# Row tiles and raw weights in buffers of their own, and the second pair's weights split on VectorE

## The chip, the cores and the metric

The kernel runs on one core of a Trainium2 chip. The metric is the device time of one execution in microseconds (us), the median of three runs. The engines are called as in the profile: PE (TensorE matmuls), PEld (TensorE weight loads), DVE (VectorE), ACT (ScalarE), POOL (GpSimd) and SP (SyncE, here only a queue that issues DMAs). "L739" is line 739 of the kernel before; the changed kernel is two or three lines longer from L475 on, so that its L742 is the same line.

## The reference

One layer of a hybrid decoder on 1024 tokens of 1024 channels, all float32. What is computed first matters here:

```python
h = rms_norm(x, pre_mix_norm[l])
proj = h @ w_in[l]
z, xbc, dt_raw, sb_qkv, nsa_q, nsa_kv, nsa_gate, merge_gate = jnp.split(proj, split_points(), axis=-1)
```

with

```python
y = xf * lax.rsqrt(jnp.mean(xf * xf, axis=-1, keepdims=True) + NORM_EPS)
```

Behind it come three token mixers (a state space scan, a stick-breaking attention and a sparse attention), a gated sum, an output projection, a second RMS norm and a gated feed-forward network (FFN) with a short causal convolution:

```python
x = x + rms_norm(mixed @ w_out[l], post_mix_norm[l])
h = rms_norm(x, pre_ffn_norm[l])
u = causal_dwconv(h @ ffn_w_up[l], ffn_conv_w[l], ffn_conv_b[l])
f = (jax.nn.gelu(gate, approximate=True) * val) @ ffn_w_down[l]
```

## The kernel before, in words

**Products in two parts.** Every float32 operand of a large product is split into a rounded high part (`ACT Copy` into a float32r tile, names ending in `hi`) and a low rest (a `subtract` on DVE or POOL, names ending in `lo`). A product is three matmuls: high by high, high by low, low by high.

**The start.** The tokens are worked in two halves h = 0, 1 of 512. SP loads the columns of x (`x<-in_xT`, channels on partitions, eight tiles of a half), the first two chunks of token-major weights (`traw<-in_wtm`, four parts each) and the eight row tiles of x (`row_load`, `uhi<-in_xr` and `ulo<-in_xr`, 128 tokens of 1024 channels each), which serve only for the sums of squares: ACT squares a row tile in place with a running sum (`square`, L483). Four row tiles make the factor 1/rms of one half (`factor`; `rt` and `rb` on ACT and DVE), which PE transposes into a bank (`factor_rows`, four 128x128 matmuls on `rb`). DVE multiplies the half's columns by it (`norm`, L544), ACT rounds (`high`, L547) and DVE subtracts (`low`, L550). Meanwhile PE makes the token-major products of half 0 from columns that carry only the channel gain (`four_tiles`); `hooks` places the transposes between these matmuls: half 0's at (k, n) = (3, 0) of the second chunk, half 1's at (7, 2). Then come the products of half 1, which need its normed columns. These parts are pinned to the order in which they are written.

**Gate unit and pairs.** Next come one gate unit (`load_w`, 128 output channels, L301 to L308) and 24 units of the state space mixer in twelve pairs (`ssm_units`). A pair is done with seven products instead of eight (a Strassen scheme): `weights7` loads two raw weight tiles of 128x1024 (`wraw`, rows a11|a12 and a21|a22), and builds from them the high and low parts of seven combinations: `whi, wlo` (products 1 and 2), `ahi, alo` (product 4), and the sums `uf`, rounded to `uhi, ulo` (products 3 and 6, 5 and 7). `eng` says which engine does the eight adds and subtracts: the gate unit and the first pair use DVE, all other pairs POOL. On the other operand, `combos` makes four sums of the normed columns for each k (DVE, L695 to L698), and 16 splits round them (ACT, L738) and subtract (DVE, L739): products 6, 7, 5 and 4 in this order. The banks are named `dense` (two), `ps_s` (two), `ps_t` (two), `ps_o` and `ps_b`. A pair's results are combined on DVE (L769 to L780), run through a four-tap convolution (ACT L341, DVE L345 and L347), a SiLU (ACT L760), and stored (`s_d<-o`).

**Buffers.** The raw weight tile is taken in turn from two buffers of the pool `w` and one of a pool that the caller gives (`turn`, L655 to L659): two of three come from `w`, the third from `wx`. Load_w uses the two of `w` as well. The same counter runs on in the FFN, where the units from 5 on are pairs again and then the down projection uses `weights7`. A DMA into a buffer waits until its last reader is through; SP issues in order, so a DMA that waits holds all behind it.

**What sets the order.** Apart from the pinned start, a scheduler with a timing model places the instructions on each engine when the kernel is built; `issue_after` (through `behind`) keeps an instruction behind a given other.

## Time and profile before

| what | value |
| --- | --- |
| median of 3 runs | 2199.31 us (2198.98 to 2203.28) |
| profiled execution, its own time | 2196.05 us |
| span of the profiled execution | 2194.3 us |
| PE busy | 2142.0 us, 98% of the span |
| DVE, ACT, POOL busy | 1349.8, 1207.4, 1212.0 us |
| granted TensorE clock | 0.996 of full speed on average |
| PE busy from 0 to 50 us, 50 to 100, 100 to 150 | 43.64, 47.45, 47.92 us |
| the same from 150 to 200 us, 200 to 250, 250 to 300 | 50.00, 49.63, 49.78 us |

The span is what the profiler sees from the first instruction to the last; the execution's own time holds 1.75 us more (2196.05 less 2194.3). A row of a timeline gives the start, the duration, the engine and line, the operation with `out<-in`, and, in brackets, the idle time of the engine ahead of it and what ended it. A list of waits gives us in total, times, and the longest.

### The profile page before, as it was taken

How to read it: one execution, taken by the hardware profiler on the slowest of the kernel's cores; microseconds unless marked ns; L12 is line 12 of the kernel's file. 1: busy time of each engine (PE TensorE's matmuls, PEld its weight loads, DVE VectorE, ACT ScalarE, POOL GpSimd, SP SyncE). 2: the span in 40 equal slices, each digit the busy share in tenths (PEclk: the TensorE clock that was granted, in tenths of full speed). 3: DMA queues.
4: the chain of work that ended last, by engine and by line, in shares of the span. 5: the costliest groups of instructions: out<-in, count | busy, mean ns of one | idle time of the engine just before them, and what ended most of it. 6: DMA issues, size and time to landing. Idle time of an engine off the chain costs nothing.

```text
span 2194.3 us, 30439 instructions
## 1 busy us (share of the span) xinstructions
PE 2142.0 (98%) x10701; PEld 1714.8 (78%) x10701; DVE 1349.8 (62%) x2492; ACT 1207.4 (55%) x2286; POOL 1212.0 (55%) x1075
## 2 busy tenths in 40 slices
PE   8999999999999999999999999999999999999997
PEld 8777879866676678888877777887788888878886
DVE  7855554256656515566547877328776767676776
ACT  6544443457857745676775554236555544475634
POOL 0566642146746743443335686648777777766733
PEclk9999999999999999999999999999999999999999
DMA  7233342321121011212336432335322323255432
GB/s 262 79 114 110 113 130 66 101 77 39 53 78 39 18 57 39 77 54 95 126 116 218 155 104 78 118 113 193 110 82 77 111 96 120 97 194 175 149 116 106
DMA packets 127562, 233.55 MB, mean 106 GB/s; under 512 B 29840, under 2 KB 43952, under 8 KB 127408
## 3 DMA queue, kind: packets, MB, share of 16 engines
q1 hardware_dynamic: 124720, 229.02, 31.6%
q10 hardware_dynamic: 2688, 2.59, 0.3%
q8 instruction: 84, 1.38, 0.3%
q14 instruction: 70, 0.57, 0.1%
HBM read 170.11 MB, written 61.44 MB: 106 GB/s over the span
## 4 chain that ended last, share of the span: by engine, by line
PE 79%; DVE 7%; ACT 5%; issue 4%; DMA 3%; POOL 2%; SPq 0%; DVEq 0%; ACTq 0%; POOLq 0%
PE dense L235 51%; PE ps_s L235 10%; PE ps_t L235 6%; PE ps_o L235 6%; PE ps_b L235 4%; PE psn L235 3%; DMA ulo<-in_xr 1%; ACT wT L1145 1%; DVE u L345 0%; DVE mx L1117 0%; POOL wlo L308 0%; DVE o L345 0%; DVE o L347 0%; DVE x L1826 0%; DMA lo<-m_d 0%
## 5 line engine op out<-in xcount | busy, mean ns | idle before, releaser
L308 POOL TENSOR_TENSOR wlo<-wraw,whi 128x256 fp32r<-128x256 f32 x300 | 238.1, 825 | 212.5 <-ACT whi L303 202.4
L235 PE MATMUL dense<-h_hi,whi 128*128 128x512 f32 x656 | 264.0, 402 | 2.1 <-DVE kk L912 2.1
L235 PE MATMUL dense<-h_hi,wlo 128*128 128x512 f32 x656 | 257.3, 392 | 0.0
L235 PE MATMUL dense<-h_lo,whi 128*128 128x512 f32 x656 | 257.2, 392 | 0.0
L1156 POOL TENSOR_TENSOR wT_lo<-wT,wT_hi 128x512 fp32r<-128x512 f32 x132 | 168.2, 1288 | 70.9 <-ACT wT_hi L1155 56.7
L235 PE MATMUL dense<-x,uhi 128*128 128x512 f32 x600 | 191.7, 391 | 1.9 <-ACT x L748 1.9
L235 PE MATMUL dense<-hi,wlo 128*128 128x512 f32 x448 | 176.4, 395 | 0.1
L235 PE MATMUL dense<-lo,whi 128*128 128x512 f32 x448 | 174.9, 391 | 1.1 <-POOL lo L1845 1.1
L235 PE MATMUL dense<-hi,whi 128*128 128x512 f32 x448 | 174.7, 390 | 0.4 <-ACT whi L303 0.4
L675 POOL TENSOR_TENSOR ulo<-uf,uhi 128x1024 fp32r<-128x1024 f32 x36 | 87.1, 2420 | 116.5 <-ACT uhi L674 116.5
L235 PEld LDWEIGHTS dense<-h_hi,wlo 128*128 128x128 f32 x656 | 123.5, 188 | 27.2 <-POOL wlo L666 0.2
L235 PEld LDWEIGHTS dense<-h_hi,whi 128*128 128x128 f32 x656 | 124.0, 189 | 25.4 <-issue 2.5
L235 PEld LDWEIGHTS dense<-h_lo,whi 128*128 128x128 f32 x656 | 123.9, 189 | 22.9
L303 ACT ACTIVATE whi<-wraw 128x1024 fp32r<-128x1024 f32 x76 | 80.4, 1058 | 111.1 <-PE dense L235 87.4
L235 PEld LDWEIGHTS dense<-x,uhi 128*128 128x128 f32 x600 | 112.4, 188 | 27.3 <-ACT x L748 3.2
L1379 POOL TENSOR_TENSOR s_lo<-sa,s_hi 128x512 fp32r<-128x512 f32 (+2 forms) x48 | 53.9, 1124 | 132.6 <-ACT s_hi L1378 132.6
L345 DVE SCALAR_TENSOR_TENSOR u<-dense,pv,u 128x510 f32<-128x510 f32 (+1 forms) x140 | 103.5, 742 | 32.3 <-ACT u L341 32.1
L1117 DVE TENSOR_REDUCE mx<-ps_t 128x1 f32<-128x384 f32 (+3 forms) x192 | 97.9, 519 | 35.2 <-PE ps_t L235 33.5
L1145 ACT ACTIVATE wT<-ps_s 128x512 f32<-128x512 f32 x132 | 78.3, 596 | 53.0 <-PE ps_s L235 48.6
L678 POOL TENSOR_TENSOR ulo<-uf,uhi 128x1024 fp32r<-128x1024 f32 x36 | 86.6, 2404 | 31.4 <-ACT uhi L677 29.9
L235 PE MATMUL dense<-x,ulo 128*128 128x512 f32 x264 | 103.2, 391 | 0.0
L666 POOL TENSOR_TENSOR wlo<-wraw,whi 128x1024 fp32r<-128x1024 f32 x36 | 88.3, 2455 | 24.3 <-ACT whi L665 24.2
(584 smaller groups left out, 6172.1 us busy)
## 6 DMA issues: line engine op xcount, KB each, us to landing
wraw<-in_wfm SPq DMA_DIRECT2D x62, 512.0 KB, 3.8
wraw<-in_wup SPq DMA_DIRECT2D x48, 512.0 KB, 3.7
lo<-m_d SPq DMA_DIRECT2D x58, 256.0 KB, 3.3
g_d<-gate_e SPq DMA_DIRECT2D x48, 256.0 KB, 2.0
s_d<-o SPq DMA_DIRECT2D x48, 256.0 KB, 2.1
m_d<-u SPq DMA_DIRECT2D x44, 256.0 KB, 2.0
row<-g_d SPq DMA_DIRECT2D x36, 256.0 KB, 3.9
row<-s_d SPq DMA_DIRECT2D x32, 256.0 KB, 5.0
```

The source lines that it names most:

```text
L235: return pin(f(*a, **k), in_order)
L303: act(hi, raw, AF.Copy)
L308: eng.tensor_tensor(lo[:, s], raw[:, s], fl(hi[:, s]), op=OP.subtract)
L345: V.scalar_tensor_tensor(o[:, d:], ps[:, :512 - d], taps[d], o[:, d:], op0=OP.mult, op1=OP.add)
L666: eng.tensor_tensor(wlo, raws[0], fl(whi), op=OP.subtract)
L675: eng.tensor_tensor(l24, f24, fl(h24), op=OP.subtract)
L678: eng.tensor_tensor(l31, f31, fl(h31), op=OP.subtract)
L1117: V.tensor_reduce(mx[:, h, a, n:n + 1], pm[:, :w], axis=AX, op=OP.max)
L1145: act(w.rearrange("p h q -> p (h q)"), pz, AF.Exp)
L1156: P.tensor_tensor(lo, wf, fl(hi), op=OP.subtract)
L1379: (P if SB_SLO else V).tensor_tensor(s_lo[:, c0:], a[:, c0:], fl(s_hi[:, c0:]), op=OP.subtract)
```

## The change

Four things are edited, and the scheduler places the rest anew.

1. **Row tiles.** The eight row tiles went to `uhi` and `ulo` in turn (two buffers each), so that rows 4 to 7 waited for the squares of rows 0 to 3. Now rows 0 and 1 go to `uhi`, 2 and 3 to `ulo`, 4 to `uf0`, 5 to `uf1`, 6 to the `wraw` of the pool wx0, and only row 7 takes a used `uhi`.
2. **Raw token-major weights.** `TM_RAW`, the number of their buffers, goes from 3 to 5; the tile `q_out`, which took room in the same pool, is gone, and its two uses take `ulo` and `uhi`. The fourth part of chunk 1 is loaded ahead of row 7 and not behind it. Its split on ACT and DVE stands ahead of the squares of rows 6 and 7, which moved into `first_rows`; the hook of half 1's transposes goes from (7, 2) to (7, 0).
3. **Second pair's weights.** For the second pair (u0 = 4) `weights7` runs on DVE and not on POOL, and behind the last of the 16 splits, whose subtracts are now in `lows`.
4. **Ring.** `turn` is set to 2 behind the first pair, so that the second pair's first raw tile takes the buffer of wx0. The counter is one lower from there on, in the FFN too.

```diff
-TM_RAW = 3
+TM_RAW = 5
...
-        x = wx0.tile([128, DM], F32, name=("uhi", "ulo")[t // 2 % 2])
+        name = ("uhi", "uhi", "ulo", "ulo", "uf0", "uf1", "wraw", "uhi")[t]
+        x = wx0.tile([128, DM], F32, name=name, bufs=2 if name in ("uhi", "ulo") else 1)
...
-        if t in (3, 7):
+        if t in (3, 6):
             with tc.issue_after(loads[-1].ins):
-                raw1.append(tm_raw(1, 2 + t // 4, tmw))
+                raw1.append(tm_raw(1, t // 3 + 1, tmw))
...
-    def q_tile(name=None):
-        if name:
-            return wx0.tile([128, DM], F32, name=name).rearrange("p (t c) -> p t c", t=4)
-        return tmw.tile([128, 4, 256], F32, name="q_out", bufs=1)
+    def q_tile(name):
+        return wx0.tile([128, DM], F32, name=name).rearrange("p (t c) -> p t c", t=4)
...
     def first_rows():
         rows.append(factor_rows(rb, ps_s))
-        for k in range(4):
+        for k in range(3):
             norm(0, k)
         chunk_weights(1, 3)
+        norm(0, 3)
+        for t in (6, 7):
+            square(t)
         late.append(factor(1)[1])
         norm(0, 4)
...
-    qs = [q_tile()]
+    qs = [q_tile("ulo")]
...
-    for t in range(4, 8):
+    for t in (4, 5):
         square(t)
-    pss = four_tiles(1, tm1, 0, (ps_o, ps_d, ps_d, ps_b), {(3, 0): first_rows, (7, 2): second_rows})
+    pss = four_tiles(1, tm1, 0, (ps_o, ps_d, ps_d, ps_b), {(3, 0): first_rows, (7, 0): second_rows})
...
-    qs.append(q_tile())
+    qs.append(q_tile("uhi"))
...
             first_w = weights7(wx, A["wfm"][U_SSM], A["wfm"][U_SSM + 1], 512, V)
+        turn[0] = 2
...
-                V.tensor_tensor(lo, t, fl(hi), op=OP.subtract)
+                lows.append(V.tensor_tensor(lo, t, fl(hi), op=OP.subtract))
...
-            with behind(columns_in, highs[-1]) if q == 0 else nullcontext():
-                w = weights7(wx, A["wfm"][U_SSM + u0], A["wfm"][U_SSM + u0 + 1], 512) if u0 else first_w
+            with behind(columns_in, highs[-1], lows[-1]) if q == 0 else nullcontext():
+                w = weights7(wx, A["wfm"][U_SSM + u0], A["wfm"][U_SSM + u0 + 1], 512, V if u0 == 4 else P) if u0 else first_w
```

On ACT, in the start, behind the transposed factor `rb` of half 0: before, four squares (`uhi` and `ulo` hold row tiles) and then the split of the last part of chunk 1 (`thi`):

```order
L517 ACTIVATE rb<-rt 128x512
L483 ACTIVATE uhi,stat<-uhi 128x1024 x2
L483 ACTIVATE ulo,stat<-ulo 128x1024 x2
L416 ACTIVATE thi<-traw 128x512
L269 ACTIVATE rt<-stat,eps 128x4
L271 ACTIVATE rt<-rt 128x4
L517 ACTIVATE rb<-rt 128x512
```

and now (`uf_161`, `uf_163` and `wraw` hold the row tiles 4, 5 and 6):

```order
L518 ACTIVATE rb<-rt 128x512
L484 ACTIVATE uf_161,stat<-uf_161 128x1024
L484 ACTIVATE uf_163,stat<-uf_163 128x1024
L416 ACTIVATE thi<-traw 128x512
L484 ACTIVATE wraw,stat<-wraw 128x1024
L484 ACTIVATE uhi,stat<-uhi 128x1024
L269 ACTIVATE rt<-stat,eps 128x4
L271 ACTIVATE rt<-rt 128x4
L518 ACTIVATE rb<-rt 128x512
```

The split moved ahead of the last two squares; nothing else moved on ACT there.

On DVE, behind the 16 splits of the pairs' columns (L739, now L742), before:

```order
L739 TENSOR_TENSOR x<-x 128x512 x16
L744 CAST rtab<-tab 128x256
L769 TENSOR_TENSOR ps_s<-ps_s,x 128x512
L343 COPY halo<-ps_s 128x3
L345 SCALAR_TENSOR_TENSOR o<-ps_s,pv,o 128x511
L345 SCALAR_TENSOR_TENSOR o<-ps_s,pv,o 128x510
L345 SCALAR_TENSOR_TENSOR o<-ps_s,pv,o 128x509
L777 TENSOR_TENSOR x<-ps_t,x 128x512
L778 TENSOR_TENSOR ps_o<-ps_o,x 128x512
```

and now (`wlo`, `uf_1082`, `uf_1083` and `alo` are the second pair's weights):

```order
L742 TENSOR_TENSOR x<-x 128x512 x16
L747 CAST rtab<-tab 128x256
L668 TENSOR_TENSOR wlo<-wraw,whi 128x1024
L673 TENSOR_TENSOR uf_1082<-wraw 128x512
L678 TENSOR_TENSOR uf_1082<-wraw 128x512
L772 TENSOR_TENSOR ps_s<-ps_s,x 128x512
L674 TENSOR_TENSOR uf_1083<-uf_1082,wraw 128x512
L675 TENSOR_TENSOR uf_1083<-uf_1083,wraw 128x512
L343 COPY halo<-ps_s 128x3
L345 SCALAR_TENSOR_TENSOR o<-ps_s,pv,o 128x511
L780 TENSOR_TENSOR x<-ps_t,x 128x512
L682 TENSOR_TENSOR alo<-wraw,ahi 128x512
```

Six of the second pair's eight operations stand between the splits and the first pair's combination and convolution; the other two (`ulo`) follow further down, one behind the convolution of `ps_o` and one ahead of that of `dense`.

On POOL, at the head of its work, before (`uf_1082` and `uf_1083` are the second pair's sums, `uf_1220` the third's):

```order
L671 TENSOR_TENSOR uf_1082<-wraw 128x512
L676 TENSOR_TENSOR uf_1082<-wraw 128x512
L672 TENSOR_TENSOR uf_1083<-uf_1082,wraw 128x512
L666 TENSOR_TENSOR wlo<-wraw,whi 128x1024
L673 TENSOR_TENSOR uf_1083<-uf_1083,wraw 128x512
L666 TENSOR_TENSOR wlo<-wraw,whi 128x1024
L680 TENSOR_TENSOR alo<-wraw,ahi 128x512
```

and now:

```order
L668 TENSOR_TENSOR wlo<-wraw,whi 128x1024 x2
L682 TENSOR_TENSOR alo<-wraw,ahi 128x512
L673 TENSOR_TENSOR uf_1220<-wraw 128x512
L678 TENSOR_TENSOR uf_1220<-wraw 128x512
L674 TENSOR_TENSOR uf_1221<-uf_1220,wraw 128x512
```

The second pair's operations are gone from POOL; it begins with the `wlo` of the third and of the fourth pair. On PE the first pair's product 4 (`ps_o<-x,ahi`, on the last four splits) and its product 6 (`dense<-x,uhi`) now follow product 7 (`ps_t<-x,uhi`) at once; before, most of the second pair's product 1 stood ahead of them, and the second pair's product 2 among them. In the FFN the first pairs' raw tiles also change places: unit 5's second tile now comes from the pool `w` behind the single units' weights, where before it came from `wx`; the four sums of unit 5 on POOL stand behind the last single unit's `wlo`, where the first of them had stood ahead of 24 of these.

## Prediction

> **What bounds the kernel now.** I read the page's busy times first, then the list of PE's waits and the chain of waits over the first 300 us (all edits but the ring lie there), then the timelines of SP, ACT, DVE, POOL and PE. The page:
>
> ```profile
> PE 2142.0 (98%) x10701; PEld 1714.8 (78%) x10701; DVE 1349.8 (62%) x2492; ACT 1207.4 (55%) x2286; POOL 1212.0 (55%) x1075
> ```
>
> PE bounds the whole. The change removes no matmul, so it can win only idle time of PE: 52 us in the span, of which the places it touches hold a few. PE's waits up to 260 us (total, times, longest):
>
> ```profile
> PE dense L235 <- ACT x L748: 2.5, 3, 1.3
> PE ps_s L235 <- ACT rb L517: 1.8, 1, 1.8
> ```
>
> The second lies in the start; of the first, 0.77 lies at the first pairs, beside two waits for DVE that are shown below.
>
> The chain of waits in the start (start, duration, what):
>
> ```profile
> 12.52 8.75 DMA ulo<-in_xr
> ...
> 22.47 5.78 DMA ulo<-in_xr
> ...
> 28.28 1.15 ACT ulo L483 x2
> 29.43 0.53 ACT thi L416
> ...
> 29.98 0.70 DVE tlo L417
> ...
> 31.23 0.71 PE dense L235 x6
> ...
> 33.00 0.45 PE ps_s L235 x4
> ...
> 33.48 2.06 DVE x L544 x3
> ```
>
> So the end of the row stage hangs on row 7 (landed 28.25), its square, then the split of the last weight part (1.2 us on ACT and DVE), which PE needs, and the transposes at 33.00, behind half of k = 7. From there the norm at 33.48 leads to PE's first matmul of half 1:
>
> ```profile
> 34.94 0.39 PE L235 MATMUL ps_t<-thi,h_hi 128*128 128x256 f32 x1 [0.80 <-ACT h_hi L547]
> ```
>
> That is 1.46 us behind the norm's start. I measure the first term there.
>
> **Term 1, row tiles and raw buffers.** SP's row for rows 4 and 5:
>
> ```profile
> 18.48 1.61 SPq L449 DMA_DIRECT2D uhi<-in_xr  x2
> ```
>
> Rows 4 and 5 were held to 18.48 by the squares of rows 0 and 1, and rows 6 and 7 behind them by those of 2 and 3; now they are issued as soon as earlier transfers land. But the transfers are near their limit (last column GB/s):
>
> ```profile
> 8.00:10.00 2.00, 2.00 (x19) 2.00 (x18) 2.00 (x4) 1.64 (x4) 0.00 (x0) 1.00 1.00 368
> 14.00:16.00 2.00, 2.00 (x19) 2.00 (x19) 0.75 (x2) 0.55 (x1) 0.00 (x0) 1.00 1.01 296
> ```
>
> Behind row 3 (landed 21.27) come weight part 3, rows 4 to 6, part 4 and row 7: 2.6 MB, 7.1 us at 368 GB/s, so row 7 lands no earlier than about 27.3 to 28.2 even when dips like the one to 296 are filled. What is won is the order on ACT. `rb` of both halves, and PE's transposes of half 0:
>
> ```profile
> 23.64 0.63 ACT L517 ACTIVATE rb<-rt 128x512 f32<-128x512 f32 x1
> 31.51 0.63 ACT L517 ACTIVATE rb<-rt 128x512 f32<-128x512 f32 x1 [1.13 <-DVE rt L274]
> 25.03 0.63 PE L235 MATMUL ps_s<-ident,rb 128*128 128x128 f32 x4 [1.83 <-ACT rb L517]
> ```
>
> I let rows 0 to 3 come 0.4 us earlier (0 to 0.7, the dip at 14 to 16: 72 of 368 GB/s over 4 us), so ACT is free at 23.9. Squares 4 and 5 (1.15 us each by the row at 28.28, and a tenth between) end near 26.4, part 4 is there at about 26.5, its split and squares 6 and 7 end near 29.5, and `rb` of half 1 follows in 1.9 us (2.7 from 29.43 to 32.14, less 0.8 of the split on ACT and DVE) at 31.4. PE, no longer held by that split, goes from its transposes at 24.6 through 48 matmuls of 0.118 to k = 7 at 30.7 and waits 0.7 us; the transposes end near 31.9 and the norm starts there, against 33.48. Term 1: **1.5 us** won. Bounds: 0.2 when part 4 lands only at 27.7 and both squares queue behind its split; 2.5 when everything lands early and PE waits for nothing. I take the value nearer the upper one because ACT's seven squares and splits, not the transfers, come out last. The hook's move costs nothing unless `rb` is late: then all of k = 7 (12 matmuls, 1.4 us) is behind the wait and not half of it; this is in the 0.2. Both `q_out` uses now hold a buffer of `ulo` and `uhi` until they are stored. The last store (ACT, issued near 58) must land before the first pair's second `uhi`; by the rows it takes 4.0 us, which makes ACT 1 to 2 us late there, most of it hidden by the idle 1.26 us ahead of the gate's sigmoid. Without that cover the splits' high parts come 2 us later, which term 2's bound holds.
>
> ```profile
> q_d<-uhi ACTq DMA_DIRECT2D x1, 512.0 KB, 4.0
> 64.44 0.60 ACT L277 ACTIVATE gate_e<-dense 128x512 f32<-128x512 f32 x1 [1.26 <-PE dense L235]
> ```
>
> **Term 2, the second pair's weights.** On POOL they ran through DVE's 16 splits:
>
> ```profile
> 67.18 5.30 POOL L671 TENSOR_TENSOR uf<-wraw 128x512 f32<-128x512 f32 x1 [66.67 <-DVE ulo L678]
> 80.37 2.83 POOL L666 TENSOR_TENSOR wlo<-wraw,whi 128x1024 fp32r<-128x1024 f32 x1
> 65.87 1.23 DVE L678 TENSOR_TENSOR ulo<-uf,uhi 128x1024 fp32r<-128x1024 f32 x1
> 67.61 3.70 DVE L739 TENSOR_TENSOR x<-x 128x512 fp32r<-128x512 f32 x6
> 71.75 14.42 DVE L739 TENSOR_TENSOR x<-x 128x512 fp32r<-128x512 f32 x10 [0.43 <-ACT x L738]
> 74.22 1.14 ACT L738 ACTIVATE x<-x 128x512 fp32r<-128x512 f32 x2
> 75.26 1.05 ACT L665 ACTIVATE whi<-wraw 128x1024 fp32r<-128x1024 f32 x1
> ```
>
> Alone, six splits take 3.70 us, 0.62 each; with POOL at work, ten take 14.42, 8.2 us too long. POOL's first add took 5.30 us, until DVE had paused at 71.3. From there they take turns, one whole instruction each. The Trainium skill's page "SBUF — State Buffer", section "Who interferes with whom", says that a DVE instruction with two SBUF inputs and a GpSimd one that reads SBUF exclude each other for the whole instruction, whichever issues first; the trace agrees, with splits of 1.4 us on average here.
>
> PE paid for it three times:
>
> ```profile
> 81.88 0.39 PE L235 MATMUL ps_s<-h_lo,whi 128*128 128x512 f32 x1
> 83.81 0.49 PE L235 MATMUL ps_o<-x,ahi 128*128 128x512 f32 x1 [1.54 <-DVE x L739]
> ...
> 96.20 0.39 PE L235 MATMUL dense<-x,ulo 128*128 128x512 f32 x1
> 97.60 0.47 PE L235 MATMUL ps_o<-x,ahi 128*128 128x512 f32 x1 [1.00 <-DVE o L345]
> ...
> 100.21 0.39 PE L235 MATMUL ps_o<-x,alo 128*128 128x512 f32 x1
> 101.37 0.50 PE L235 MATMUL dense<-h_hi,uhi 128*128 128x512 f32 x1 [0.77 <-ACT x L748]
> ```
>
> A matmul here starts 0.23 us behind the one ahead, so these starts are 1.70, 1.17 and 0.93 late: 3.8 us. In the changed order, in times of before (term 1 taken off): ACT's high parts set the pace of the splits up to the 12th, near 75.4. POOL's only operation then is the third pair's `wlo` (2.83 in turns, some 2.4 alone as the `ulo` below), which starts behind `whi` near 76.3 and blocks one split; the 13th ends near 79.4, the 16th near 81.2, against 86.2. Product 4 now stands right behind product 7 and wants the 13th near 78.8 and one more split every 0.7 us: it waits 0.65 us. By the row at 67.18, where POOL waited out six splits, DVE would lose nothing and PE wait 0; at the worst the splits slip by the 2 us above and PE waits 2.6.
>
> Behind the splits DVE has the eight operations: 3 of 1024 columns at 1.23 us and 5 of 512 at 0.62, 6.8 us, of which six stand ahead of the convolutions. Counting on in steps of 0.6 to 0.75, `wlo` ends at 82.7 (PE wants it at 85.2, behind products 4 and 6), the first combination at 84.5, the convolution of `ps_s` at 89.7 and of `ps_o` at 92.0. PE, 12 matmuls or 2.75 us for a product, wants `ps_s` again at 92.4 and `ps_o` at 95.2. So these 6.8 us lie beside PE's work with 2.7 and 3.2 us to spare; without that cover each is a us of PE for a us of DVE. The convolutions read PSUM and do not take turns with POOL: this `ulo` of 2.40 us and this convolution of 0.75 lie over each other, and neither is longer than elsewhere.
>
> ```profile
> 101.78 2.40 POOL L675 TENSOR_TENSOR ulo<-uf,uhi 128x1024 fp32r<-128x1024 f32 x1
> 102.90 0.75 DVE L345 SCALAR_TENSOR_TENSOR o<-ps_t,pv,o 128x511 f32<-128x511 f32 x1 [0.25 <-ACT o L341]
> ```
>
> Term 2: 3.8 less 0.65, **3.15 us** won (1.2 to 3.8).
>
> **Term 3, the ring.** Each raw tile takes the buffer of the third one before it, before and now; only the phase shifts, and the second pair's first tile waits for the first pair's second instead of the gate's, two us apart and long before use. In the FFN the second tile of unit 5 loses the free buffer and is loaded behind the single units:
>
> ```profile
> 1543.12 1.83 SPq L660 DMA_DIRECT2D wraw<-in_wup  x1
> 1605.97 0.33 SPq L660 DMA_DIRECT2D wraw<-in_wup  x1
> 1613.46 2.93 POOL L2030 TENSOR_TENSOR x<-x,lo 128x512 fp32r<-128x512 f32 x2 [1.23 <-DVE x L2030]
> ```
>
> It was issued at 1543, and now near 1608, behind the store at 1608; it lands near 1612 (3.64 us such a load takes at 132.45, quoted below). Three sums of 1.29 (as at 131.14, below) then hold POOL to 1615.9, and the two splits behind them start 2.4 us later than 1613.46. On PE 12 matmuls (2.7 us) moved ahead of the product that wants them, so I cost it at **0.2 us** lost (a gain of 0.5, since POOL has one sum less among the single units, to 2.5 without that cover).
>
> **Sum.** 1.5 + 3.15 - 0.2 = 4.45 us. The profiled span 2194.3 becomes 2189.85, its execution 2196.05 becomes 2191.6. The median is 3.26 above the profiled execution, so it becomes 2199.31 - 4.45 = **2194.8 us**.
>
> **The rivals.**
>
> *The transfers and POOL keep what they had.* Term 1 falls to 0.2 because the bytes are the same, and the third pair's `wlo` with the late store costs term 2 its worst, 1.2: 2199.31 - 1.4 + 0.2 = 2198.1. For it speak 296 to 368 GB/s through the start; against it that only one POOL operation is left. In this case the change mostly doesn't do what it says.
>
> *The FFN gives it back.* Term 3 at 2.5: 2197.2. For it, the chain through L2030; against it, the matmuls moved ahead.
>
> *DVE becomes the bound: slower.* Place: DVE from the 16th split to the convolution of `ps_o`. Each of the eight moved operations reads SBUF twice and can be blocked by POOL, as splits were; at 1.7 us for each (8.2 us over the five that the five POOL operations behind 72.43 blocked) DVE is 13.4 us late, less 2.7 to spare is 10.7 lost on PE: 2199.31 - 4.45 + 10.7 = 2205.6. It is slower from the point where DVE is 7.2 us late (2.7 and the 4.45). Against it: POOL has two `wlo` and an `alo` in that stretch, not eight operations.
>
> *More is won.* A gap of 1.3 us near 147 comes from a raw tile:
>
> ```profile
> 131.14 1.29 POOL uf L673
> ...
> 132.45 3.64 DMA wraw<-in_wfm
> ```
>
> POOL has a pair's work less ahead of this; if ACT's wait for that tile goes, with 0.65 of term 2's wait: 2194.8 - 1.95 = 2192.9. Against it: the sums wait for a buffer that PE's product 3 frees, and so move with PE.
>
> **How the numbers follow.** Forecast 0.53, transfers and POOL 0.17, FFN 0.10, DVE 0.08, more 0.12. About 0.2% (4.4 us, so 2194.9) is what a measurement of this kernel can tell from no change. The forecast, with its own range of 2193 to 2197, lies on that bound, so half of it, 0.27, and all of "more", with some of the FFN's, make 0.42 for faster; 0.08 of DVE and 0.02 for chance make 0.10 for slower; 0.48 is left for the same. The range of 2191.5 to 2199.0 leaves out the slower case and the ends.
>
> **What would show it.** Right: no wait of POOL's or DVE's at half 1's norm beyond 32.5; the 16 splits in 11 to 14 us and not 18.5; the three late starts down to one below 1 us; PE's product 3 of the first pair near 96.5 and not 101.37. Wrong: row 7 landing later than 28.2; splits of 2.9 us in a row; `ps_s` or `ps_o` waited for by PE behind DVE's `ulo` or convolution; PE idle near 1618 to 1626.

## The result, and the profile after

The changed kernel takes **2188.51 us** (median of 4 runs, 2187.56 to 2190.49) against 2199.52 for the kernel before (4 runs, 2198.98 to 2203.28): a ratio of **0.9947, 95% interval 0.993 to 0.9965**, 11.0 us less. Forecast were 2194.8 with a range of 2191.5 to 2199.0: the sign is right, and 6.3 us more were won than predicted. The changed kernel's profiled execution took 2189.08 us, 6.97 less than the profiled one of before (2196.05).

The page of the changed kernel, its span and PE's share:

```profile
span 2187.4 us, 30438 instructions
...
PE 2139.8 (98%) x10701; PEld 1713.4 (78%) x10701; DVE 1344.8 (61%) x2500; ACT 1208.2 (55%) x2286; POOL 1192.7 (55%) x1067
```

PE is busy for 2.2 us less than before (2142.0), and the span is 6.9 us shorter: most of the gain is idle time of PE that is gone. The list of PE's waits in the first 330 us (us in total, times, longest):

```profile
PE dense L235 <- DVE kk L915: 2.1, 1, 2.1
PE ps_s L235 <- ACT h_hi L495: 1.3, 1, 1.3
PE dense L235 <- DVE eps L259: 1.1, 1, 1.1
PE dense L235 <- ACT x L751: 0.8, 2, 0.6
PE ps_t L235 <- DVE h_lo L549: 0.7, 1, 0.7
PE ps_s L235 <- issue: 0.6, 1, 0.6
```

The waits on a split, on a convolution and on half 1's `h_hi` have left the list, and the wait on the copies of `dense` (`x`) went from 2.7 to 0.8. Ahead of half 0's transposes PE idles for 0.64 instead of 1.83 (the row that ends in `issue`; 0.97 and 0.80 in the changed kernel's second and third profile, 0.88 in the fourth of before). DVE's timeline shows half 1's norm (predicted at 31.9, before 33.48), the 16 splits and the first of the moved operations:

```profile
30.61 2.06 DVE L543 SCALAR_TENSOR_TENSOR x<-x,pv,ps_s 128x512 f32<-128x512 f32 x3 [0.81 <-PE ps_s L235]
...
64.75 3.69 DVE L742 TENSOR_TENSOR x<-x 128x512 fp32r<-128x512 f32 x6
...
74.00 4.30 DVE L742 TENSOR_TENSOR x<-x 128x512 fp32r<-128x512 f32 x4 [0.69 <-ACT x L741]
...
78.43 1.21 DVE L668 TENSOR_TENSOR wlo<-wraw,whi 128x1024 fp32r<-128x1024 f32 x1
```

The splits take 13.5 us instead of 18.5. One of the last four is blocked, 4.30 us where four alone take some 2.5, by POOL's only operation in that stretch, the third pair's `wlo`, as predicted. PE starts the first pair's product 3 without a wait, at 94.77 (before 101.37, forecast about 96.5):

```profile
94.77 0.40 PE L235 MATMUL dense<-h_hi,uhi 128*128 128x512 f32 x1
```

The lead over the kernel before is 2.9 us at half 1's first products (32.30 against 35.16), 6.6 at product 3, 7.8 near 150, still 8.0 in front of the FFN, and 6.6 at the last matmul: up to there more was won than forecast, and behind it some was given back.

### The profile page after: what moved, and what is told of

The parts are those of the page before. It is cut to its first block, busy times and chain, and to the rows that moved or that the text cites. A ratio compares the mean times of both kernels' runs of the same rounds, so it can differ in the third digit from the quotient of the medians.

```text
span 2187.4 us, 30438 instructions
## 1 busy us (share of the span) xinstructions
PE 2139.8 (98%) x10701; PEld 1713.4 (78%) x10701; DVE 1344.8 (61%) x2500; ACT 1208.2 (55%) x2286; POOL 1192.7 (55%) x1067
## 4 chain that ended last, share of the span: by engine, by line
PE 83%; DVE 6%; ACT 4%; issue 4%; POOL 1%; DMA 1%; SPq 0%; DVEq 0%; ACTq 0%; POOLq 0%
PE dense L235 53%; PE ps_s L235 11%; PE ps_t L235 6%; PE ps_o L235 6%; PE ps_b L235 4%; PE psn L235 3%; ACT wT L1148 1%; POOL wlo L308 0%; DVE mx L1120 0%; DVE x L1829 0%; DVE u L345 0%; DMA traw<-in_wtm 0%; ACT wT_hi L1158 0%; DVE x L2027 0%; DMA wraw<-in_wo 0%
## 5 line engine op out<-in xcount | busy, mean ns | idle before, releaser
L677 POOL TENSOR_TENSOR ulo<-uf,uhi 128x1024 fp32r<-128x1024 f32 x35 | 84.1, 2404 | 105.0 <-ACT uhi L676 101.7
L680 POOL TENSOR_TENSOR ulo<-uf,uhi 128x1024 fp32r<-128x1024 f32 x35 | 84.2, 2405 | 38.3 <-ACT uhi L679 29.3
```

The costliest lines, as they stand in the source:

```text
L677: eng.tensor_tensor(l24, f24, fl(h24), op=OP.subtract)
L680: eng.tensor_tensor(l31, f31, fl(h31), op=OP.subtract)
```

## Experiments

Each variant was timed beside the kernel before on one chip; that gave 95 executions of it with a median of 2199.13 us (2193.79 to 2206.48). The changed kernel has 16 (2187.56 to 2192.87, median 2189.30). A ratio is to the kernel before in the same comparison. "The last sum" is the last matmul on `osq`, just ahead of the FFN. One profile each, in us:

| kernel | half 1's norm | from there to product 3 | to the last sum | to the last matmul |
| --- | --- | --- | --- | --- |
| before | 33.48 | 67.89 | 1442.76 | 636.42 |
| before, second to fourth profile | 34.06, 33.29, 31.73 | 68.00, 67.77, 67.91 | 1444.76, 1448.69, 1442.74 | 636.36, 636.81, 636.72 |
| start only | 30.30 | 67.90 | 1442.56 | 636.60 |
| second pair only | 31.81 | 64.13 | 1440.96 | 637.11 |
| phase only | 32.02 | 67.85 | 1441.37 | 639.49 |
| order of the start only | 33.83 | 67.76 | 1444.32 | 636.60 |
| changed, old order of the start | 32.16 | 64.28 | 1442.08 | 638.73 |
| changed, second pair on POOL | 30.57 | 67.96 | 1442.38 | 638.95 |
| changed, no phase | 31.63 | 64.15 | 1442.50 | 637.32 |
| changed, phase put back (two) | 30.40, 30.95 | 64.74, 64.14 | 1441.10, 1440.42 | 636.82, 636.93 |
| changed (three) | 30.61, 30.92, 30.91 | 64.16, 64.14, 64.11 | 1441.33, 1441.24, 1440.93 | 637.89, 638.32, 638.55 |

The second column is the cleanest: 67.8 to 68.0 where the second pair is as before, 64.1 to 64.7 where it is on DVE, whatever else changes.

### Start only

The kernel before with items 1 and 2 of the change:

```diff
             first_w = weights7(wx, A["wfm"][U_SSM], A["wfm"][U_SSM + 1], 512, V)
-        turn[0] = 2
...
-                w = weights7(wx, A["wfm"][U_SSM + u0], A["wfm"][U_SSM + u0 + 1], 512, V if u0 == 4 else P) if u0 else first_w
+                w = weights7(wx, A["wfm"][U_SSM + u0], A["wfm"][U_SSM + u0 + 1], 512) if u0 else first_w
```

(against the changed kernel; the marks on the splits go, too)

> The kernel before with the start's part of the change alone: row tiles and raw tiles in buffers of their own, the last weight part split ahead of squares 6 and 7, the hook at (7,0); the second pair's weights stay on GpSimd and the ring's phase as it was. Theory A (two stages that add up; the first term was simply sized too small): half 1's norm starts near 30.6 us, 2.9 earlier than 33.48, and the same 2.9 is there at the first pair's product 3 (98.5 against 101.37); the wait of 1.3 us near 147 stays; 2.9 us less than before, about 2196.6. Theory B (the transfers and the alternation of the splits with GpSimd take the early start back): the norm near 30.6, but the splits end near 86 as before and product 3 is within 1 us of 101.37; 2199 us.

Measured: 2196.12 us, ratio 0.9982 (0.9971 to 0.9993), 2.9 us less. The norm stands at 30.30, product 3 at 98.20, and the waits near 81, 95, 98 and 145 are all there (1.54, 1.05, 0.81, 1.34). Theory A.

### Second pair only

The kernel before with item 3:

```diff
-                V.tensor_tensor(lo, t, fl(hi), op=OP.subtract)
+                lows.append(V.tensor_tensor(lo, t, fl(hi), op=OP.subtract))
...
-            with behind(columns_in, highs[-1]) if q == 0 else nullcontext():
-                w = weights7(wx, A["wfm"][U_SSM + u0], A["wfm"][U_SSM + u0 + 1], 512) if u0 else first_w
+            with behind(columns_in, highs[-1], lows[-1]) if q == 0 else nullcontext():
+                w = weights7(wx, A["wfm"][U_SSM + u0], A["wfm"][U_SSM + u0 + 1], 512, V if u0 == 4 else P) if u0 else first_w
```

> The kernel before with the second pair's weights alone changed: on VectorE, behind the splits. The start and the ring's phase stay. Theory A (the second term is 3.7 us at product 3 and takes the 1.3 us near 147 with it, because GpSimd runs a pair's work earlier): norm at 33.5, the 16 splits in about 14 us, product 3 at 97.6, no wait near 147; 5.0 us less than before, about 2194.5. Theory B (the wait near 147 goes by the ring's phase): product 3 at 97.6, but the wait near 147 stays at about 1.3; 3.7 us less, 2195.8. Theory C (the second term needs the earlier start): product 3 near 100, 2198.

Measured: 2190.84 us, ratio 0.9956 (0.9943 to 0.9969), 8.1 us less where theory A had 5.0 and the prediction 3.15. Product 3 comes 3.75 us sooner behind the norm, and the wait near 147 is down to 0.22 (at 141.23). The mechanism of A holds; its size in the times does not.

### No phase, and the phase put back

```diff
-        turn[0] = 2
```

> The changed kernel without the shift of the raw ring's phase, all else as it is. Theory A (the phase does nothing for the first pairs and costs the feed-forward stage about 1.3 us): norm at 30.6, product 3 at 94.8, no wait near 147, and the lead over the kernel before, 7.9 us from 150 on, is still above 7.5 at the end instead of 6.6; 1.2 us below the changed kernel, 2187.3. Theory B (the phase takes the wait near 147): the wait of 1.3 is back near 140; 2188.5 to 2189.8.

```diff
     ssm_units()
+    turn[0] += 1
```

> The changed kernel with the raw ring's counter one higher behind the state-space units, so that the first pairs have the changed phase and the feed-forward stage has the one of before. Theory A (the late 1.3 us are the phase's): the lead of 7.9 us at 150 is 7.3 or more at the end, and the wait on GpSimd's low part near 1532 and the one near 1617 are as in the kernel before; 2187.3. Theory B (the late loss is scatter of loads from DRAM, not the phase): waits of the same size at other places; 2188.5.

Measured: 2188.92 us (0.9952, 0.9937 to 0.9967) and 2188.61 us (0.995, 0.9935 to 0.9966). Without the phase the wait near 147 stays away (0.22), so DVE's taking over the second pair is enough to remove it. From the last sum to the end both need 637.3 or less, as before: the time lost late is the phase's.

### The kernel before and the changed kernel again

> The kernel before, unchanged, for a second profile and more executions. Theory A (its trace is the same from execution to execution and the scatter of 2194 to 2206 us is the granted clock, which falls to half for some 3.4 us behind idle time of TensorE): half 1's norm at 33 to 34, the splits end at 85 to 87, product 3 at 100.5 to 102, the wait of 1.3 near 147, at equal clock a time within 2 us of the first profile's. Theory B (the alternation of the splits with GpSimd differs from one execution to the next, and that is the scatter): the end of the splits moves by more than 2 us.

> The changed kernel, unchanged, for a second profile and more executions beside those of the kernel before. Theory A (part of the difference of medians, about 2 to 4 of 11 us, is a higher mean granted clock, since fewer stretches fall to half behind idle time): mean clock 0.996 to 0.997 against 0.995 of the kernel before; at equal clock 6 to 8 us apart. Theory B (the clock differs by chance): mean clocks within 0.0005 of each other, and the medians 6 to 8 us apart.

Measured: 2198.59 us (ratio 0.9995, 0.9981 to 1.0008) and 2189.47 us (0.9956, 0.9941 to 0.9971). The splits end at 86.73 (86.17 in the first profile) and product 3 starts at the same distance from the norm. But the wait near 147 has doubled, and behind it PE runs at half speed. PE's timeline of the kernel before, second profile (two matmuls in a row of x2 start 0.23 us apart at full clock):

```profile
146.57 0.63 PE L235 MATMUL ps_t<-x,uhi 128*128 128x512 f32 x2
149.84 1.22 PE L235 MATMUL dense<-x,uhi 128*128 128x512 f32 x2 [2.64 <-ACT x L748]
150.85 0.63 PE L235 MATMUL ps_t<-x,ulo 128*128 128x512 f32 x1
151.28 1.06 PE L235 MATMUL ps_t<-x,uhi 128*128 128x512 f32 x2
```

and the same stretch in windows of 2 us, the granted clock third from the end of a row:

```profile
148.00:150.00 2.00, 0.16 (x1) 0.17 (x1) 2.00 (x4) 1.11 (x2) 2.00 (x3) 0.78 0.00 0
150.00:152.00 2.00, 2.00 (x5) 1.63 (x6) 2.00 (x4) 0.58 (x1) 1.92 (x2) 0.50 0.35 131
152.00:154.00 2.00, 2.00 (x6) 1.54 (x6) 1.93 (x4) 0.82 (x2) 0.44 (x1) 0.50 0.02 7
154.00:156.00 2.00, 2.00 (x7) 1.54 (x6) 0.64 (x2) 0.00 (x0) 0.00 (x0) 0.51 1.24 282
156.00:158.00 2.00, 2.00 (x10) 1.64 (x9) 1.32 (x3) 0.63 (x1) 0.00 (x0) 1.00 0.79 297
```

The matmuls of `ps_t` start 0.43 us apart. Summed over windows of 1 us, 3.42 us are lost to the clock here, beside the wait of 2.64: together 6.1 us, where the execution of which the prediction saw the profile has 1.3. Of these 4.8 us more, 4.1 arrive: PE is 0.69 us behind the first profile at the matmul of 145.87 (145.18 there) and 4.80 at that of 155.97 (151.17 there). Neither theory A (all scatter is clock) nor B (the splits) is quite right: the scatter has both a wait that differs and a clock that follows it.

Why the wait is there at all shows in the first profile of before. DVE's timeline, a convolution's last step on the halo:

```profile
144.66 1.95 DVE L347 SCALAR_TENSOR_TENSOR o<-halo,pv,o 128x3 f32<-128x3 f32 x1
```

POOL's timeline beside it:

```profile
144.19 2.40 POOL L678 TENSOR_TENSOR ulo<-uf,uhi 128x1024 fp32r<-128x1024 f32 x1 [0.91 <-ACT uhi L677]
```

and ACT's, the SiLU and the copy that PE wants:

```profile
146.65 0.63 ACT L760 ACTIVATE o<-o 128x512 f32<-128x512 f32 x1 [1.86 <-DVE o L347]
147.18 0.58 ACT L748 ACTIVATE x<-dense 128x512 f32<-128x512 f32 x1
```

The operation on 3 columns, where the one on 2 columns ahead of it took 0.21, ends 0.02 us behind POOL's subtract: it was blocked like a split. (In the variants without this wait it starts just ahead of the subtract and takes 0.21: at 142.66 against 142.70 with the phase alone, at 138.38 against 138.70 with the second pair alone.) The SiLU waits for it, and the copy stands behind the SiLU. In the second profile POOL blocks the halo operation of one tap earlier (145.17, 2.13 us), one more step of the convolution (0.73) and the last halo operation (0.76) come behind it, and the copy starts at 149.20. The prediction had named the late raw tile for this wait; its last link is POOL against DVE again.

### Second pair back on POOL, behind the splits

```diff
-                w = weights7(wx, A["wfm"][U_SSM + u0], A["wfm"][U_SSM + u0 + 1], 512, V if u0 == 4 else P) if u0 else first_w
+                w = weights7(wx, A["wfm"][U_SSM + u0], A["wfm"][U_SSM + u0 + 1], 512) if u0 else first_w
```

> The changed kernel with the second pair's weights back on GpSimd, but still behind the splits. It tells what the engine does from what the place does. Theory A (the engine matters: GpSimd needs 1.3 us where VectorE needs 0.62, and 2.4 where it needs 1.23, 12.5 us against 6.8): the splits end at 78 to 79 as in the changed kernel, but the second pair's product 6 (86.5 in the changed kernel) and product 3 of the first pair wait for the weights; 3 us above the changed kernel, 2191.5. Theory B (only the place matters, GpSimd being out of the splits' way): product 3 at 94.8 and the time as in the changed kernel, 2188.5. Theory C (the weights come much later than PE wants them, 6 us or more lost): 2195.

Measured: 2193.62 us, ratio 0.9975 (0.9965 to 0.9985), 4.2 above the changed kernel in that comparison. The outcome is of theory A's size, by another mechanism: POOL is not behind the splits at all, since the marks keep an order on one engine only. POOL's timeline:

```profile
64.27 5.29 POOL L673 TENSOR_TENSOR uf<-wraw 128x512 f32<-128x512 f32 x1 [63.77 <-DVE ulo L680]
69.52 1.75 POOL L678 TENSOR_TENSOR uf<-wraw 128x512 f32<-128x512 f32 x1
...
77.47 2.83 POOL L668 TENSOR_TENSOR wlo<-wraw,whi 128x1024 fp32r<-128x1024 f32 x1
```

and DVE's:

```profile
68.85 14.40 DVE L742 TENSOR_TENSOR x<-x 128x512 fp32r<-128x512 f32 x10 [0.44 <-ACT x L741]
```

The splits end at 83.3, as late behind the norm as before (67.96 to product 3). The change of engine is what takes POOL out of the splits. The wait near 147 is 0.22 here, though the second pair is on POOL: here it is the phase that removes it.

### Phase only

```diff
             first_w = weights7(wx, A["wfm"][U_SSM], A["wfm"][U_SSM + 1], 512, V)
+        turn[0] = 2
```

> The kernel before with the shift of the raw ring's phase alone. The wait near 147 went in the kernel with the phase and the second pair on GpSimd, and also in the two with VectorE and without the phase, so either of the two parts is enough to take it. Theory A (that holds): the splits and product 3 as before (86 and 101.4 to 102.1), the wait near 147 down to 0.3 or less; 1.3 us less by the wait, and up to 1.5 more where the clock fell to half behind it: 2196 to 2197.7. Theory B (the phase needs the earlier start): the wait stays; 2199.

Measured: 2197.58 us, ratio 0.9991 (0.9982 to 1.0). The splits are as before, the wait near 147 is 0.22, and 639.49 us go from the last sum to the end. Theory A: either the phase or DVE's taking over removes that wait, and the phase costs behind it.

### The start's two parts apart

The changed kernel with the old order:

```diff
-        for k in range(3):
+        for k in range(4):
             norm(0, k)
         chunk_weights(1, 3)
-        norm(0, 3)
-        for t in (6, 7):
-            square(t)
...
-    for t in (4, 5):
+    for t in range(4, 8):
         square(t)
-    pss = four_tiles(1, tm1, 0, (ps_o, ps_d, ps_d, ps_b), {(3, 0): first_rows, (7, 0): second_rows})
+    pss = four_tiles(1, tm1, 0, (ps_o, ps_d, ps_d, ps_b), {(3, 0): first_rows, (7, 2): second_rows})
```

> The changed kernel with the old order of the start's work: squares 4 to 7 ahead of the second chunk, the last weight part split behind the fourth norm, the hook at (7,2). Row tiles and raw tiles keep their own buffers. Theory A (the earlier rows carry the first term): half 1's norm at 31 to 31.5, at most 0.9 later than 30.6; time 2189.3. Theory B (the order carries it, the buffers next to nothing): norm at 32.5 or later; time 2190.5 or more.

and the kernel before with the new order (the same lines the other way):

> The kernel before with the new order of the start's work alone: squares 6 and 7 behind the split of the last weight part and the fourth norm, the hook at (7,0). Row tiles and raw tiles share their buffers as before. With the old order in the changed kernel half 1's norm stood at 32.16 us, with both parts at 30.6 to 30.9, with neither at 33.5 to 34.1. Theory A (the two parts add up, 1.3 to 1.9 for the buffers and 1.3 to 1.5 for the order): norm at 32.0 to 32.7, about 1.4 us less than before, 2197.6. Theory B (the order is worth nothing without the earlier rows, since squares 6 and 7 wait for rows that land at 27 to 28): norm at 33.3 or later, 2199.

Measured: 2193.41 us (0.9976, 0.9965 to 0.9988), norm at 32.16; and 2198.49 us (0.9996, 0.9987 to 1.0006), norm at 33.83. The order alone is worth nothing, but for another reason than theory B gives. ACT's timeline of it:

```profile
28.49 0.63 ACT L416 ACTIVATE thi<-traw 128x512 fp32r<-128x512 f32 x1 [2.51 <-DMA traw<-in_wtm]
```

The split, now ahead of two squares, holds them for a raw part that still lands late: the order needs the raw tile's own buffer. The buffers without the order leave the norm at 32.16 where both give 30.3 to 31.6; with starts that scatter by over 1 us and one profile, the order's share is near 1.4 us and not better known. The norm of 32.16 lies between the two theories of the first of these runs, and its time in theory B's range.

### Filling PE's idle time

The changed kernel with matmuls of ones in two idle stretches:

```diff
+FILL = 9
...
+        if s == 0:
+            with tc.issue_after(E.last_ssm.ins), tc.issue_after(E.mms[-1].ins):
+                for _ in range(FILL):
+                    last = mm(ph[:, :128], E.ones, E.ones, start=True, stop=True)
...
+            if q == 0 and c == 0:
+                with tc.issue_after(E.mms[-1].ins):
+                    for _ in range(FILL):
+                        mm(bank[:, :128], E.ones, E.ones, start=True, stop=True)
```

> The changed kernel with nine matmuls of ones in each of two idle stretches of TensorE, 2.12 us near 310 and 2.07 near 1149, into banks that are written over afterwards; they compute nothing that is used. Theory A (the granted clock falls to half for 3.4 us, 1.71 us lost each time, because TensorE was idle just before): no stretch at half clock behind these two places, where 4 and 5 of 10 profiles had one; mean granted clock up by about 0.0007 from 0.9969, and 1.0 to 1.5 us less, 2187.5 to 2188. Theory B (the clock falls for another reason, at about these times): stretches at half clock there as before, and the time as the changed kernel's, 2189, or above.

Measured: 2189.86 us, ratio 0.9957 (0.9943 to 0.997), mean clock 0.9974 over 5 executions. The stretches are filled (a matmul of ones counts as two):

```profile
307.56 2.17 PE L238 MATMUL ps_o<-ones 128*128 128x128 f32 x18
309.85 0.47 PE L238 MATMUL dense<-h_hi,whi 128*128 128x512 f32 x1
```

and the clock stays at 1.00 behind both. But it is halved from 324 to 331 in this profile, behind 32 matmuls of 64 columns, and the time is no better: 1.7 us ahead of the changed kernel's first profile at 315, it is 2.7 behind at 331 and 1.7 at the last matmul. So the clock at the two places fits theory A and the time does not; that a stretch which came in 4 and 5 of 10 profiles is missing from one decides little.

Why nothing is won near 310 shows without any filling, in two profiles of the changed kernel. The clock is halved from 311.28 to 314.70 in the first and not at all there in the second, and PE goes from 0.35 us ahead of the second (307.51 against 307.86) to 1.22 behind it (314.63 against 313.41). These are PE's next matmuls on `kk`, in the first and in the second:

```profile
321.93 3.72 PE L235 MATMUL ps_o<-w,kk 128*127 128x64 f32 x32
322.25 3.76 PE L235 MATMUL ps_o<-w,kk 128*127 128x64 f32 x32 [1.46 <-DVE kk L915]
```

The first is 0.32 us ahead again: the slow stretch only took the place of a wait for DVE's `kk`. Clock that is lost is not always time that is lost.

The same at the start of the kernel before:

```diff
+FILL = 7, 3, 3
...
+                    fill(ps, FILL[1])
+                    tm_products(ps, ci, ws, 4 * h + n, k, partial(fill, pss[3], FILL[2]))
...
     def factor_rows(rb, bank=ps_b):
         r = bank()
+        if not rows:
+            fill(r, FILL[0])
```

> The kernel before with matmuls of ones in three idle stretches of TensorE at the start (7 in the wait for the first factor near 25, 3 each in the two waits near 35 and 36), into banks that are written over afterwards; they compute nothing that is used, and the waits themselves stay as long. Over the kernels so far the mean granted clock was 0.9949 with the old start and 0.9962 with the new one (second pair's place alike). Theory A (the clock falls to half in some executions because of those idle stretches, which the new start shortens): mean clock up by about 0.0010 to 0.9958, and 2 us less than the kernel before, 2197. Theory B (the clock's mean has another cause): clock 0.9948, 2199.

Measured: 2202.66 us, ratio 1.0021 (1.0008 to 1.0034), mean clock 0.9944. The first filling failed:

```profile
24.41 1.83 PE L236 MATMUL ps_s<-ones 128*128 128x128 f32 x14 [1.54 <-DVE q_out L543]
26.07 0.60 PE L236 MATMUL ps_s<-ident,rb 128*128 128x128 f32 x4
```

The bank was still being read, so PE idled as before and did the filling behind it. There is no sign of theory A's gain (the time is above that of before), but the idle time of 1.54 was not taken away, so it decides nothing on that; the wait near 147 is 2.65 here.

### Two more profiles of the kernel before

> The kernel before, unchanged, for a third profile. Theory A: every stretch at half clock stands behind idle time of TensorE of over 1 us or behind matmuls with few columns, each costs 1.7 us or a multiple, and their number accounts for the difference to the profile of 2196.05 us within 1.5 us; the waits near 25, 84, 98 and 147 are there again, the one near 147 of 1.3 or 2.6. Theory B: the difference lies in work that takes longer at full clock.

> The kernel before, unchanged, for a fourth profile; as for the third. Theory A: stretches at half clock behind the waits near 25, 36 or 147 in at least one of the two profiles. Theory B: none at these places in either.

Measured: 2202.02 and 2194.57 us. In the third profile the wait near 147 is 2.64 (at 148.85), with 1.67 us lost to the clock behind it, and 5.1 us are lost between 333 and 343, behind a wait of 1.43 and the matmuls of 64 columns. In the fourth it is 1.31 with no loss behind it, and 5.1 us are lost at three later places. The clock's share is 3.4, 6.8, 6.8 and 5.1 us in the four, which leaves 2192.6, 2191.9, 2195.2 and 2189.5 at full clock. So theory A's bound of 1.5 us is missed by both (2.6 above the first, 3.1 below): the wait near 147 makes 1.3 of the one and an earlier norm 1.75 of the other. Of the expected stretches behind 25, 36 or 147 the third profile has one.

The sum itself is at fault, too, since it takes every loss of clock for time. In the fourth profile the clock is halved from 1135.77 to 1139.18, in the first it is not; PE is 1.62 us ahead of the first profile at 1126.56 and 1.64 at 1141.68, and the wait of 1.13 on `w_hi` that the first has at 1142.52 is missing in the fourth. Its 1.48 us less come from the earlier norm, and not from the clock.

### The phase in the times

> The changed kernel with the ring's counter put back one step behind the state-space units, a second time and beside the changed kernel on one chip. In nine profiles with the ring's old phase the time from the last sum of squares ahead of the feed-forward stage to the last matmul was 636.4 to 637.3 us, in six with the shifted phase 637.6 to 639.5. Theory A (the shift costs the feed-forward stage 1.7 us, not 0.2): that time at 636.4 to 637.3, and 1 to 2 us less than the changed kernel. Theory B (no difference that can be measured): within 0.7 us of it.

> The changed kernel, unchanged, beside the one with the counter put back. Theory A: 637.6 to 638.5 us from the last sum of squares to the last matmul, 1 to 2 us above the other. Theory B: the medians within 0.7 us. Mean granted clock 0.996 to 0.997 again, against 0.995 of the kernel before.

Measured: 2188.21 us (0.9951, 0.9936 to 0.9965) against 2189.43 (0.9956, 0.9941 to 0.9971), and 636.93 us against 638.55 from the last sum to the end. Over all comparisons the medians are 2188.61 (11 executions) and 2189.30 (16). Every profile with the shifted phase needs more from the last sum to the end (637.6 to 639.5) than any with the old one (636.4 to 637.3); in the times the two kernels are not told apart. No variant beats the changed kernel by more than can be measured.

## Why the prediction was wrong, point by point

Averaged over four profiles of before and three of the changed kernel, the stages give 2.3 (norm), 3.75 (to product 3), 3.6 (to the last sum) and -1.7 us (to the end), 8.0 together; the timed medians of the large samples are 9.8 apart.

- **The baseline: this step failed most.** "The median is 3.26 above the profiled execution" was carried over as a constant. It was scatter of the kernel before, and part of it goes with the waits that the change removes: the changed kernel's three profiled executions (2189.08, 2189.56, 2189.66) lie within 0.4 us of the median of its 16 (2189.30), the four of before (2196.05, 2198.71, 2202.02, 2194.57) on both sides of its own (2199.13). The forecast for the profiled execution was 2191.6 and is off by 2.5; the other 3.8 of the 6.3 come from this step.
- **The wait near 147.** It stood among the rivals ("more is won") at 1.3 us, from one profile. The mechanism came true. Its size was not to be had from one profile: with the wait there it was 1.31, 2.64, 2.64, 1.31, 1.34 and 2.64 in the six profiles of the kernels before, start only and order only, and behind two of the three long ones the clock was halved (3.42 and 1.67 us). On average that is 2.8 us, if all of that clock is time. The sum had no term for the stretch from product 3 to the last sum, where 3.6 us are won on average and 1.4 in the pair of profiles shown. The argument against it, that the sums move with PE, fell: not the sums' start but POOL's subtract over DVE's halo operations decides.
- **Term 2 to product 3**: 3.75 us for 3.15. The DVE part held step by step: ACT sets the pace, one split is blocked, 13.5 us. The 0.65 charged to PE was not paid in the changed kernel's three profiles; it was paid, 0.69, in one of the two with the phase put back, where the matmuls stand in the same order but the splits take 14.2 us. The fear that DVE becomes the bound had nothing to it: its operations end in time for both convolutions, with no wait of PE's. (That rival's 13.4 us are not its own eight times 1.7, which is 13.6; its time would be 0.2 us more.)
- **Term 1**: 1.5 forecast (0.2 to 2.5), 2.87 in the pair of profiles shown, 2.3 on average, since the norm of before scatters from 31.7 to 34.1. Two parts of it were mis-sized. Rows 0 to 3 were to come 0.4 us earlier; in this pair row 3 lands at 20.06 instead of 21.27 and `rb` of half 0 is made at 22.43 instead of 23.64, 1.2 earlier (half 0's transposes 0.7 on average). Before, SP held the weight part ahead of the rows until 10.72, for DVE's last `tlo` on its buffer; with five buffers it goes out at 8.59. And the 0.7 us that PE was to wait for half 1's `rb` was not paid: PE comes to the transposes at 29.96 with no idle time ahead of them. The transfers are not at the limit that the rival feared, nor at the prediction's bound of 27.3 for row 7, which ACT squares from 26.85 without a wait. SP's queue issues the rows 0 and 1 and the rows 4 to 6 at

```profile
9.17 1.46 SPq L450 DMA_DIRECT2D uhi<-in_xr  x2
...
12.97 1.00 SPq L450 DMA_DIRECT2D uf<-in_xr  x2
14.30 0.33 SPq L450 DMA_DIRECT2D wraw<-in_xr  x1
```

  where it stood at 11.10, 18.48 and 21.19 before, and ACT makes half 1's `rb` at 29.23 instead of 31.51.
- **Term 3**: 0.2 lost was forecast (0.5 gained to 2.5 lost), 1.6 to 1.7 is lost. POOL needs 1.65 to 1.74 us for each of unit 5's sums and not 1.29, so that PE waits for `wlo` in spite of the 12 matmuls moved ahead. PE's timeline of the changed kernel, and of the one with the phase put back:

```profile
1614.55 0.50 PE L235 MATMUL dense<-hi,wlo 128*128 128x512 f32 x1 [0.29 <-POOL wlo L668]
1617.34 0.50 PE L235 MATMUL dense<-hi,uhi 128*128 128x512 f32 x1 [0.65 <-ACT snap L1863]
...
1961.10 0.50 PE L235 MATMUL dense<-hi,fhi 128*128 128x512 f32 x1 [1.09 <-ACT fhi L2103]
```

  and

```profile
1618.51 0.50 PE L235 MATMUL dense<-hi,uhi 128*128 128x512 f32 x1 [0.53 <-ACT snap L1864]
...
1959.94 0.50 PE L235 MATMUL dense<-hi,fhi 128*128 128x512 f32 x1 [0.41 <-ACT fhi L2104]
```

  These waits are 1.1 us longer, which is all that the two profiles differ by from the last sum to the end (637.89 against 636.82); 0.4 of it is unit 5's. The rest, 0.7, is in the down projection's first units, which take their raw tiles from the same two buffers and which the prediction did not look at; ACT makes this `fhi` behind other work of its own, and how the shift gets there is not shown.

**What stays open.** The mean granted clock was 0.9948 over the 95 executions of before and 0.9968 over 16 of the changed kernel: 0.0020 of 2190 us, 4.4 us of clock. How much of that is time can be read at equal clock: the executions at 0.997 take 2195.35 us before (mean of 11) and 2189.03 changed (9), those at 0.996 2196.37 (12) and 2190.91 (2), those at 0.995 2198.52 (24) and 2192.63 (2). So 5.5 to 6.3 of the 9.8 us are there at equal clock, and the rest, some 4, comes with a clock that is halved less often. The profiles show some of it behind the start's wait (1.71 us of clock once in four, of which 0.7 reaches half 1's products) and behind the wait near 147. That the rest, too, follows from the waits removed is argued, not shown: both fillings decide little, and the changed kernel with the old order had a mean of only 0.9950 over 12 executions without either of the waits near 84 and 147.

## What to carry to other kernels

A single profile is one draw: where the timed runs lie above it, ask which waits vary before the distance is carried over as a constant, and give a wait that stands in one profile a price with a spread. Clock that was lost counts as time only where PE's next wait does not shrink by as much. Where GpSimd and VectorE both read SBUF, look for the small VectorE operations that a long GpSimd subtract blocks, not only for the long ones; taking the GpSimd work away from that stretch helps at places that no one listed. A counter that hands out buffers has to be followed to the end of the program when its phase is shifted.

## What the runs showed of the hardware

**The granted clock falls to half in pieces of one size.** In the 18 profiles of these kernels, up to the last matmul, the clock is halved for 3.41 us (1.71 us of clock) or for two or three times that. All but the fall in the filled kernel stand right behind a wait of PE's of 1.08 us or more, some of these with matmuls of 64 columns between, and the same wait is followed by it in some executions and not in others: the wait of 2.1 us on `kk` in 8 of the 17 profiles in which it was not filled. The Trainium skill's page "TensorE: Matmul & The Clock Gate" (section "HAM oscillation — how this bites in real kernels") sums its rule up as no idle gaps of PE of more than about 3.4 us. The length of the pieces agrees with the window that the page gives; the rule does not, since here waits of 1.24, 1.87 and 2.12 us were enough, and the measurement decides.

**Where a wait lies in these pieces decides.** Within a profile all falls begin a whole number of 3.413 us apart (before, second profile: 26.25, 149.13 and 323.21, 36 and 51 pieces), so the execution can be cut into such pieces. These are the pieces around the wait of 1.83 us on half 0's factor in the first profile of before and around that of 1.87 in the second (start and end, length, PE's busy time; the granted clock is third from the end):

```profile
21.48:24.89 3.41, 1.72 (x15) 1.52 (x13) 1.84 (x8) 3.24 (x7) 0.00 (x0) 1.00 0.81 294
22.84:26.25 3.41, 1.54 (x14) 1.37 (x14) 3.02 (x10) 3.31 (x7) 0.00 (x0) 1.00 0.93 293
```

Behind the first (PE busy for 50%) the clock stays, behind the second (45%) it is halved. Over the 18 profiles all 22 pieces at full clock in which such a row counts PE busy for less than 46% are followed by a halved one, 9 of the 205 with 46 to 76%, and none of the 11,189 with more. A wait of PE of 1 to 3 us can so cost up to 1.7 us more than its length, by chance of where it falls, and as little as nothing where PE would have waited again.

**A blocked operation's size does not matter.** A VectorE operation of three columns took 1.95 us beside a GpSimd subtract of 2.40 us, and 0.21 where it started just ahead of one.
